# Merging four heads at a time, three merges in flight, and a lag of four units in a dilated-attention layer on one Trainium2 core

## The chip, the cores and the metric

The kernel runs on one core of a Trainium2 chip. The metric is the device time in microseconds of one execution, and the time given is the median of several executions. TensorE is called PE in the profile's rows, VectorE DVE, ScalarE ACT, GpSimd POOL, SyncE SP; PEld is TensorE's loading of weights. All DMAs that the kernel starts are issued from SP's queue.

## The reference, cut to what matters

Two layers work on 1,024 tokens of width 1,024. The first (mixer A) is a dilated sliding-window attention with 16 heads of 64. For each of three groups (window, dilation) it computes queries, keys and values, rotates queries and keys, and takes a banded softmax over tokens strided by the dilation. The three groups' results are then merged by their softmax denominators, multiplied by a SiLU gate and projected:

```python
for gi, (window, dil) in enumerate(((128, 1), (512, 4), (2048, 16))):
    q, k, v = ...
    o, lse = banded_attention(strided(q), strided(k), strided(v), window // dil)
    outs.append(o); lses.append(lse)
wts = softmax(stack(lses), axis=0)
o = einsum('gbsh,gbshd->bshd', wts, stack(outs))
return (o * silu(z)) @ w_out
```

Then `x <- LayerNorm(alpha * x + mixer(x))` and `x <- x + sigmoid(x Wg) * (p Wp)`. The second layer (mixer B) is a sliding-window attention with shared keys and values, a learned sink per head, the same kind of gate and the same ending; it has no merge.

## The kernel before, in words

Every large product is taken as three fp16 products of high and low halves (lines 272 to 274): a tile of 128 tokens by 512 columns is 24 matmuls into one bank of PSUM (`lin`). Weight blocks are loaded (L102), measured (L109, then a 128x128 diagonal `mdd`, a matmul at L237 and a maximum) and split into halves `whl` (L132 on ScalarE, L133 on VectorE), a step at a time, between the tiles that use the block before. The block of the output projection's second half is split into `wo`, in a pool that opens when layer A's attention pool `att` has closed, on the same memory.

Layer A (`layer_a`) runs over two pairs of head quarters, and in each over the groups 1, 2, 0. A group begins with eight tiles of values (`v_out`) for eight heads, then has two blocks (`i` = 0, 1) of eight tiles of queries and keys for four heads each. A query-key tile is rotated with the group's tables `cos` and `sin` (L347, L350 on VectorE, L351 on POOL), split (L357, L358, L361) and transposed by a DMA into `qk` (L362). It then queues a *unit* of four heads: `score` (matmuls L385, masked maxima L389, exponentials L395, halves L399 and L401, a DMA transpose into `pT` at L404), and `value` (matmuls L416 to L418 into one of two halves of the PSUM tile `o`, then ScalarE's copy into `st` at L698, and a DMA of `st` to the scratch tensor `scr` in DRAM at L707). `unit_step` starts one unit's scores and computes the weighted values of the unit `lag` steps before; there are as many `pT` buffers as the lag and one more `st`. `upt` sets how many units a tile brings.

When group 0 of a head quarter pair has its values for a token tile, a `merge` is queued: it loads the three groups' results for eight heads (`gt`, L749), finds the weights from their maxima and sums (L754 to L762, with one exponential on ScalarE, L756), weighs and adds the three on POOL (L765 to L767) and VectorE (L769, L770), and writes the result to `o_dr` (L771, named `oa` in rows). At most two merges are under way, and `merge_every` says after how many tiles each advances by a step.

The gate `z` of layer A is 16 tiles (`z_tile`, L720 to L723) after the last group. Then `mixed` reads the merged rows and the gate (L898, L899), multiplies them on POOL (L902), scales, splits and transposes them (L878, `ogT`), and runs the output projection as tiles of `lin` from `ogT`.

The order of each engine's instructions is laid out ahead by a planner that plays the program on a timeline of its own (`schedule_with_timeline_sim=True`). An instruction goes where the planner thinks its inputs and buffers are ready, with the program's order as priority; each engine, and SP's queue, then takes its list in order. So a merge's loads can stand far ahead of their place in the program: the first `gt` load of the trace is issued at 261 us, when group 1 of the first pair has been written.

## Time and profile before

| what | us |
|---|---|
| median of 3 runs | 1657.37 (1656.64 to 1660.12) |
| the profiled execution | 1658.17 |
| its span, first to last instruction | 1656.4 |
| TensorE busy | 1587.8 (96%) |
| VectorE busy | 1078.1 (65%) |
| ScalarE busy | 922.7 (56%) |
| POOL busy | 664.6 (40%) |
| mean granted clock of TensorE | 0.985 of full speed |

A busy share is a mean over stages. Layer A with its gate lasts from about 75 to 1055 us, its ending to 1225, layer B the rest. A wait in the rows is named by what ended it, in brackets behind the instruction that waited; times of instructions are from the start of the span.

### The profile page before, as it was taken

What the parts mean: (1) busy time and instruction counts of PE and PEld (TensorE: products, weight loads), DVE (VectorE), ACT (ScalarE), POOL (GpSimd) and SP (SyncE); (2) the same over time, 40 slices, a digit from 0 to 9 for tenths busy, and PEclk for the clock granted to TensorE, in tenths of its full rate; (3) what the DMA queues carried; (4) which work ended last, traced back from release to release, by engine and by line L of the source; (5) the groups of instructions that cost most, each with busy time, mean ns of one, the idle gap of its engine ahead of it and who ended that gap; (6) DMA issues with size and microseconds to landing.
All of it is one profiled execution on the core that took longest, in us unless ns stands there. A gap on an engine that the chain in (4) does not pass through costs nothing. (4 is left out here: it accounts for less than half of the span.)

```text
span 1656.4 us, 29029 instructions
## 1 busy us (share of the span) xinstructions
PE 1587.8 (96%) x10579; PEld 883.2 (53%) x10579; DVE 1078.1 (65%) x2619; ACT 922.7 (56%) x2050; POOL 664.6 (40%) x477
## 2 busy tenths in 40 slices
PE   9999999999999799999999988899999998999998
PEld 3455676654555456666545543344455555544444
DVE  6866655655566776556466567887447998677731
ACT  4537665675774467656657843533334878754321
POOL 0015624532554665155235653453323452225341
PEclk9999999999999999999999998999999999999999
DMA  9718867775887777567658885989975898998963
GB/s 362 251 61 172 186 135 149 153 158 126 164 159 203 207 170 159 127 157 163 142 124 187 190 226 202 336 221 264 248 185 113 155 206 183 189 297 215 262 197 109
DMA packets 543792, 311.02 MB, mean 188 GB/s; under 512 B 473120, under 2 KB 494240, under 8 KB 543392
## 3 DMA queue, kind: packets, MB, share of 16 engines
q1 hardware_dynamic: 543648, 309.16, 75.3%
q8 instruction: 83, 1.36, 0.3%
q14 instruction: 61, 0.50, 0.1%
HBM read 137.78 MB, written 54.92 MB: 116 GB/s over the span
## 5 line engine op out<-in xcount | busy, mean ns | idle before, releaser
L272 PE MATMUL lin<-whl,xhl 128*128 128x512 f16 x1280 | 488.5, 382 | 2.6 <-ACT zu L722 2.6
L273 PE MATMUL lin<-whl,xhl 128*128 128x512 f16 x1280 | 488.7, 382 | 0.0
L274 PE MATMUL lin<-whl,xhl 128*128 128x512 f16 x1280 | 488.7, 382 | 0.0
L351 POOL TENSOR_TENSOR t<-t,t 128x512 f32<-128x512 f32 (+1 forms) x120 | 153.4, 1278 | 284.8 <-DVE t L350 268.0
L401 POOL TENSOR_TENSOR phl<-sm,phl 128x1024 f16<-128x1024 f32 (+1 forms) x88 | 155.6, 1769 | 233.3 <-ACT phl L399 205.9
L109 DVE TENSOR_REDUCE wpm<-wraw 128x1 f32<-128x1024 f32 (+1 forms) x132 | 156.8, 1197 | 93.6 <-DMA wraw<-in_wa_dram 54.8
L274 PEld LDWEIGHTS <-xhl 128*128 128x128 f16 x1280 | 149.3, 117 | 127.5 <-issue 3.5
L273 PEld LDWEIGHTS <-xhl 128*128 128x128 f16 x1280 | 149.7, 117 | 119.5 <-issue 6.7
L272 PEld LDWEIGHTS <-xhl 128*128 128x128 f16 x1280 | 149.4, 117 | 119.7 <-issue 3.8
L395 ACT ACTIVATE sm<-sm,st,cs 128x128 f32<-128x128 f32 (+1 forms) x384 | 203.6, 532 | 3.6 <-ACT st L393 0.4
L358 POOL TENSOR_TENSOR hl<-t,hl 128x512 f16<-128x512 f32 (+1 forms) x120 | 145.3, 1211 | 131.7 <-ACT hl L357 131.7
L389 DVE CUSTOM_DVE_ANT_0 sm<-s,tab 128x256 f32<-128x256 f32 (+1 forms) x512 | 157.0, 358 | 31.5 <-PE s L385 23.0
L133 DVE SCALAR_TENSOR_TENSOR whl<-wraw,s,whl 128x1024 f16<-128x1024 f32 (+1 forms) x116 | 168.3, 1501 | 12.8 <-ACT whl L132 12.8
L357 ACT ACTIVATE hl<-t 128x512 f16<-128x512 f32 (+1 forms) x120 | 72.3, 602 | 125.4 <-POOL t L351 124.0
L347 DVE TENSOR_TENSOR t<-lin,rope 128x512 f32<-128x512 f32 (+1 forms) x120 | 78.9, 657 | 75.7 <-PE lin L274 41.6
L132 ACT ACTIVATE whl<-wraw,s 128x1024 f16<-128x1024 f32 (+1 forms) x116 | 121.8, 1122 | 5.1 <-DVE s L212 5.0
L272 PE MATMUL lin<-whl,x2T 128*128 128x512 f16 (+1 forms) x320 | 115.5, 361 | 0.0
L273 PE MATMUL lin<-whl,x2T 128*128 128x512 f16 (+1 forms) x320 | 115.2, 360 | 0.0
L274 PE MATMUL lin<-whl,x2T 128*128 128x512 f16 (+1 forms) x320 | 115.0, 359 | 0.0
L399 ACT ACTIVATE phl<-sm 128x1024 f16<-128x1024 f32 (+1 forms) x128 | 110.2, 861 | 1.2
L361 ACT ACTIVATE hl<-hl 128x512 f16<-128x512 f16 (+1 forms) x104 | 63.2, 608 | 54.2 <-POOL hl L358 53.9
L385 PE MATMUL s<-qk 128*128 128x128 f16 x1120 | 81.5, 220 | 9.1 <-DMA qk<-hl 9.1
(187 smaller groups left out, 2883.5 us busy)
## 6 DMA issues: line engine op xcount, KB each, us to landing
wraw<-in_wa_dram SPq DMA_DIRECT2D x56, 512.0 KB, 6.0
scr<-st SPq DMA_DIRECT2D x96, 132.0 KB, 2.3
gt<-scr SPq DMA_DIRECT2D x48, 264.0 KB, 3.4
wraw<-in_wav_dram SPq DMA_DIRECT2D x24, 512.0 KB, 6.4
prh<-pro SPq DMA_DIRECT2D x32, 256.0 KB, 4.1
wraw<-in_wg_dram SPq DMA_DIRECT2D x16, 512.0 KB, 8.7
wraw<-in_wb_dram SPq DMA_DIRECT2D x16, 512.0 KB, 6.4
xg<-y SPq DMA_DIRECT2D x16, 512.0 KB, 3.6
```

Source lines behind the costliest of these rows:

```text
L109: k.nc.vector.tensor_reduce(pm[:, c:c + 1], self.raw[:, c * q:(c + 1) * q], axis=AX.X, op=ALU.max, apply_absolute_value=True)
L132: nc.scalar.activation(hl[:, 0, sl], self.raw[:, sl], AF.Copy, scale=self.s)
L133: self.last = nc.vector.scalar_tensor_tensor(hl[:, 1, sl], self.raw[:, sl], self.s, hl[:, 0, sl], op0=ALU.mult, op1=ALU.subtract)
L272: mm(ps, xh(kt), wh, start=(kt == 0), stop=False)
L273: mm(ps, xh(kt), wl, start=False, stop=False)
L274: mm(ps, xl(kt), wh, start=False, stop=(kt == NK - 1))
L351: nc.gpsimd.tensor_add(t1[:, :nh * HD], t1[:, :nh * HD], t2[:, :nh * HD])
L358: nc.gpsimd.tensor_sub(hl[:, :nh, HD:P], rv, hl[:, :nh, 0:HD])
L389: nc.vector.tensor_tensor_reduce(sm[:, h, :nk], ps[:, i, :nk], mask, 1.0, -3e38, ALU.add, ALU.max, mx[:, h:h + 1])
L395: nc.scalar.activation(sm[:, h, :nk], sm[:, h, :nk], AF.Exp, bias=nbias[:, h:h + 1], scale=cs, accum_out=sums[:, h:h + 1])
L399: nc.scalar.activation(hl[:, 0], sm[:, :, :nk], AF.Copy)
L401: eng.tensor_sub(hl[:, 1], sm[:, :, :nk], hl[:, 0])
```

## The change: four heads per merge, three merges, a lag of four, one rotary buffer

A merge now takes one head quarter (four heads) instead of two, so there are 32 merges with tiles of half the size, and the merges of a pair's first quarter are queued in the first of its two blocks in group 0. Three of them may be under way, and `gt` and `mw` have three buffers. Layer A's lag between scores and weighted values goes from three units to four, with one more `pT` and one more `st` buffer. The rotary tables have one buffer instead of two, and their load stands in the program behind the third value tile instead of ahead of the block.

```diff
@@ -190,7 +190,7 @@
 
     def rope_tables(self, order):
 
-        t = self.const.tile([P, N_ROPE], F32, name="rope", tag="rope", bufs=2)
+        t = self.const.tile([P, N_ROPE], F32, name="rope", tag="rope")
         self.nc.sync.dma_start(t, self.a["tab"][:, order * N_ROPE:(order + 1) * N_ROPE])
         self.cos = t[:, :NT * 32].rearrange("p (n c) -> p n c", n=NT)
         self.sin = t[:, NT * 32:].rearrange("p (n b c) -> p n b c", n=NT, b=2)
@@ -629,7 +629,7 @@
                for i in range(2)]
 
         self.x2_scale()
-        self.set_lag(3)
+        self.set_lag(4)
         self.upt = 0.75
         vh = at.tile([P, 3, NT, 4 * HD], F16, tag="vh", name="vh", bufs=1)
         vl = at.tile([P, 3, NT, 4 * HD], F16, tag="vl", name="vl", bufs=1)
@@ -640,7 +640,6 @@
             for g in (1, 2, 0):
                 if pair and g == 0:
                     self.merge_every = 1
-                self.rope_tables(g)
                 blk = self.next_block()
                 cvs[pair, g] = self.prod(self.invx, blk.inv, 2.0 ** V_SHIFT, "cv")
                 slots = [i for i in range(3) if i != slots[1]]
@@ -648,6 +647,8 @@
                 for n in range(NT):
                     ps = self.ps_lin.tile([P, 512], F32, tag="lin", name="lin")
                     self.lin(ps, blk, *self.stat_a(g, n), 0, 512)
+                    if n == 2:
+                        self.rope_tables(g)
                     self.v_out(ps.rearrange("p (s c) -> p s c", s=2), vh[:, pick, n, :], vl[:, pick, n, :])
                     self.progress()
                 blk.released = True
@@ -705,8 +706,8 @@
             else:
                 d = d[n * P:(n + 1) * P]
             nc.sync.dma_start(d, st)
-            if g == 0 and q % 2:
-                self.merges.append(self.merge(n, q // 2, scr[q // 2]))
+            if g == 0:
+                self.merges.append(self.merge(n, q, scr[q // 2]))
 
         kas = [lambda h, sw, t=qk[i]: t[:, 4 + 4 * sw + h, :] for i in tiles]
         self.later(UNIT_LAG, lambda: self.unit(lambda h: qk[n][:, h, :], kas, mask, cs, ncs,
@@ -741,35 +742,34 @@
             if half == 0:
                 self.w_z.released = True
 
-    def merge(self, n, pair, scr):
+    def merge(self, n, q, scr):
 
         nc, at, sp = self.nc, self.att, self.small
-        gt = at.tile([P, 3, 2, 4 * HD + 8], F32, tag="gt", name="gt")
+        gt = at.tile([P, 3, 4 * HD + 8], F32, tag="gt", name="gt", bufs=3)
         for g in range(3):
-            nc.sync.dma_start(gt[:, g], scr[g][n * P:(n + 1) * P])
-        sums, nb = gt[:, :, :, 4 * HD:4 * HD + 4], gt[:, :, :, 4 * HD + 4:]
+            nc.sync.dma_start(gt[:, g], scr[g][n * P:(n + 1) * P, q % 2])
+        sums, nb = gt[:, :, 4 * HD:4 * HD + 4], gt[:, :, 4 * HD + 4:]
         yield
-        w = sp.tile([P, 3, 2, 4], F32, tag="mw", name="mw")
-        M = sp.tile([P, 2, 4], F32, tag="mM", name="mM")
-        nc.vector.tensor_reduce(M, nb.rearrange("p g a h -> p a h g"), axis=AX.X, op=ALU.min)
-        nc.vector.tensor_sub(w, M.unsqueeze(1).to_broadcast([P, 3, 2, 4]), nb)
+        w = sp.tile([P, 3, 4], F32, tag="mw", name="mw", bufs=3)
+        M = sp.tile([P, 4], F32, tag="mM", name="mM")
+        nc.vector.tensor_reduce(M, nb.rearrange("p g h -> p h g"), axis=AX.X, op=ALU.min)
+        nc.vector.tensor_sub(w, M.unsqueeze(1).to_broadcast([P, 3, 4]), nb)
         nc.scalar.activation(w, w, AF.Exp)
-        wl = sp.tile([P, 3, 2, 4], F32, tag="mwl", name="mwl")
+        wl = sp.tile([P, 3, 4], F32, tag="mwl", name="mwl")
         nc.vector.tensor_mul(wl, w, sums)
-        L = sp.tile([P, 2, 4], F32, tag="mL", name="mL")
-        nc.vector.tensor_reduce(L, wl.rearrange("p g a h -> p a h g"), axis=AX.X, op=ALU.add)
+        L = sp.tile([P, 4], F32, tag="mL", name="mL")
+        nc.vector.tensor_reduce(L, wl.rearrange("p g h -> p h g"), axis=AX.X, op=ALU.add)
         nc.vector.reciprocal(L, L)
-        nc.vector.tensor_mul(w, w, L.unsqueeze(1).to_broadcast([P, 3, 2, 4]))
-        x = [gt[:, g, :, 0:4 * HD].rearrange("p a (h c) -> p a h c", c=HD) for g in range(3)]
-        wb = [w[:, g].unsqueeze(3).to_broadcast([P, 2, 4, HD]) for g in range(3)]
+        nc.vector.tensor_mul(w, w, L.unsqueeze(1).to_broadcast([P, 3, 4]))
+        x = [gt[:, g, 0:4 * HD].rearrange("p (h c) -> p h c", c=HD) for g in range(3)]
+        wb = [w[:, g].unsqueeze(2).to_broadcast([P, 4, HD]) for g in range(3)]
         nc.gpsimd.tensor_mul(x[1], x[1], wb[1])
         nc.gpsimd.tensor_mul(x[2], x[2], wb[2])
         nc.gpsimd.tensor_add(x[1], x[1], x[2])
         yield
         nc.vector.tensor_mul(x[0], x[0], wb[0])
         nc.vector.tensor_add(x[0], x[0], x[1])
-        nc.sync.dma_start(self.o_dr[n][:, pair * 512:(pair + 1) * 512].rearrange("p (a c) -> p a c", a=2),
-                          gt[:, 0, :, 0:4 * HD])
+        nc.sync.dma_start(self.o_dr[n][:, 4 * HD * q:4 * HD * (q + 1)], gt[:, 0, 0:4 * HD])
 
     def merge_step(self):
 
@@ -777,7 +777,7 @@
         if self.merge_wait > 0:
             return
         self.merge_wait = self.merge_every
-        while len(self.merging) < 2 and self.merges:
+        while len(self.merging) < 3 and self.merges:
             self.merging.append(self.merges.pop(0))
         for m in list(self.merging):
             if next(m, "end") == "end":
```

## Rows read from the trace of the kernel before

**Rows 1.** The page's first part: busy time of each engine in us, its share of the span, and its number of instructions.

```profile
PE 1587.8 (96%) x10579; PEld 883.2 (53%) x10579; DVE 1078.1 (65%) x2619; ACT 922.7 (56%) x2050; POOL 664.6 (40%) x477
```

**Rows 2.** TensorE's waits over the whole span: the instruction that waited, what it waited for, us in total, times, the longest.

```profile
PE s L237 <- DVE mdd L230: 15.6, 3, 7.3
PE s L385 <- DMA qk<-hl: 9.1, 5, 3.1
PE o L416 <- DMA pT<-phl: 8.1, 5, 3.7
PE o L416 <- ACT st L698: 7.9, 4, 4.4
```

**Rows 3.** The timeline of TensorE, its longer stalls in and behind layer A, two weighted values (975.95, 981.83) and the first projection stall of layer B: start in us, us of the instruction (or the run of equal ones), and in brackets the idle time before it and what ended that.

```profile
527.62 0.19 PE L416 MATMUL o<-vh,pT 128*128 128x64 f16 x1 [2.17 <-ACT st L698]
...
551.35 0.21 PE L416 MATMUL o<-vh,pT 128*128 128x64 f16 x1 [4.45 <-ACT st L698]
...
574.65 1.07 PE L385 MATMUL s<-qk 128*128 128x128 f16 x16 [3.12 <-DMA qk<-hl]
...
956.19 0.73 PE L385 MATMUL s<-qk 128*128 128x128 f16 x10 [1.47 <-DMA qk<-hl]
960.66 0.24 PE L416 MATMUL o<-vh,pT 128*128 128x64 f16 x1 [3.73 <-DMA pT<-phl]
...
975.95 0.19 PE L416 MATMUL o<-vh,pT 128*128 128x64 f16 x1
...
981.83 0.19 PE L416 MATMUL o<-vh,pT 128*128 128x64 f16 x1
...
1028.40 0.29 PE L237 MATMUL s<-mdd,ones 128*128 128x128 bf16 x1 [4.89 <-DVE mdd L230]
...
1054.14 0.29 PE L237 MATMUL s<-mdd,ones 128*128 128x128 bf16 x1 [7.33 <-DVE mdd L230]
1054.67 0.59 PE L272 MATMUL lin<-whl,ogT 128*128 128x512 f16 x1 [0.24 <-PE s L237]
...
1484.63 0.29 PE L237 MATMUL s<-mdd,ones 128*128 128x128 bf16 x1 [3.35 <-DVE mdd L230]
```

**Rows 4.** Windows: the stretch, its length in us, the busy us (and instructions) of PE, PEld, DVE, ACT and POOL, the granted clock of TensorE (1.00 is full speed), the DMA engines' busy share, GB/s.

```profile
505.00:590.00 85.00, 72.79 (x518) 41.45 (x517) 63.99 (x164) 38.77 (x99) 52.49 (x38) 0.94 0.73 189
...
860.00:936.00 76.00, 75.06 (x652) 42.13 (x651) 44.78 (x135) 58.68 (x146) 43.86 (x30) 1.00 0.83 168
936.00:986.00 50.00, 44.79 (x369) 24.38 (x367) 33.41 (x83) 31.53 (x72) 26.13 (x17) 0.93 0.94 235
986.00:1029.00 43.00, 35.51 (x158) 15.57 (x157) 28.21 (x59) 10.91 (x18) 18.86 (x15) 0.94 0.56 191
1029.00:1055.00 26.00, 18.43 (x74) 7.60 (x73) 18.43 (x40) 18.98 (x25) 8.42 (x6) 0.83 0.98 335
1055.00:1140.00 85.00, 79.48 (x354) 35.05 (x353) 72.44 (x149) 29.50 (x33) 39.23 (x22) 0.96 0.94 255
```

**Rows 5.** The timeline of SP's queue: the last write of `scr`, the last three loads of `gt`, the last two outputs of merges; start and us of issuing.

```profile
985.92 0.38 SPq L707 DMA_DIRECT2D scr<-st  x1
...
1007.97 1.27 SPq L749 DMA_DIRECT2D gt<-scr  x3
...
1023.95 3.42 SPq L771 DMA_DIRECT2D oa<-gt  x2
```

**Rows 6.** The timeline of ScalarE at one of the stalls of rows 3, and where `wo` opens in layer A and in layer B.

```profile
546.08 0.22 ACT L756 ACTIVATE mw<-mw 128x24 f32<-128x24 f32 x1 [2.34 <-DVE mw L755]
...
546.69 4.25 ACT L132 ACTIVATE whl<-wraw,s 128x1024 f16<-128x1024 f32 x4
550.85 0.46 ACT L698 ACTIVATE st<-o,cv 128x256 f32<-128x256 f32 x1
...
1029.40 4.26 ACT L132 ACTIVATE wo<-wraw,s 128x1024 f16<-128x1024 f32 x4 [10.74 <-DMA oa<-gt]
...
1459.83 2.19 ACT L132 ACTIVATE wo<-wraw,s 128x1024 f16<-128x1024 f32 x2 [3.96 <-DMA ob<-mu]
```

**Rows 7.** The tile `gt`: who waited for its instructions, us in total and times.

```profile
  ACT mw L756: 54.6, 14
  DVE mM L754: 27.5, 11
```

**Rows 8.** Groups of instructions by line and shape: busy us, mean ns of one, and the idle time before them with what ended it.

```profile
L351 POOL TENSOR_TENSOR t<-t,t 128x512 f32<-128x512 f32 x112 | 149.8, 1337 | 275.8 <-DVE t L350 259.9 <-DVE m L218 9.9 <-DVE mdt L226 2.7
...
L765 POOL TENSOR_TENSOR gt<-gt,mw 128x512 f32<-128x512 f32 x16 | 23.6, 1477 | 58.3 <-DVE mw L762 56.7 <-DMA gt<-scr 1.3
...
L770 DVE TENSOR_TENSOR gt<-gt 128x512 f32<-128x512 f32 x16 | 17.8, 1113 | 7.9 <-POOL gt L767 7.8
...
L755 DVE TENSOR_TENSOR mw<-mM,gt 128x24 f32<-128x24 f32 x16 | 4.8, 302 | 0.3
...
L351 POOL TENSOR_TENSOR t<-t,t 128x128 f32<-128x128 f32 x8 | 3.6, 454 | 9.0 <-DVE t L350 8.1 <-DVE inv L211 0.5 <-DVE m L218 0.4
```

**Rows 9.** DMA issues: what, from where, number, KB each, median us from issue to landing.

```profile
scr<-st SPq DMA_DIRECT2D x96, 132.0 KB, 2.3
gt<-scr SPq DMA_DIRECT2D x48, 264.0 KB, 3.4
...
rope<-in_tab_dram SPq DMA_DIRECT2D x7, 384.0 KB, 3.7
```

## The prediction

> **What bounds the kernel now.** I read the page first. TensorE is busy for 1587.8 us, 96% of the span [rows 1], so only what keeps it waiting, or slows it, can be won. The list of its waits [rows 2] has no large item: 15.6 us for the diagonal `mdd` of a weight block's maximum, 9.1 us for `qk` transposes, 8.1 us for `pT` transposes, 7.9 us for ScalarE to empty `o`. So I asked where they lie. The timeline of TensorE [rows 3] puts nearly all of layer A's into two places: 527 to 575 us, where the weighted values of the first head pair end and its merges run, and 956 to 1055 us, where the same happens for the second pair and the output projection must start. In windows [rows 4], 505 to 590 holds 85 - 72.79 = 12.2 us of idle TensorE at a granted clock of 0.94; 936 to 1055 holds 119 - (44.79 + 35.51 + 18.43) = 20.3 us at 0.93, 0.94 and 0.83. A clock under 1 means that part of the window ran at the lower level (1.2 GHz instead of 2.4), after a stall each time. Taking the missing share of the window as lost time, 505 to 590 loses another 0.06 x 85 = 5.1 us, and 936 to 1055 loses 0.07 x 50 + 0.06 x 43 + 0.17 x 26 = 10.5 us.
>
> What do these stalls have to do with merges? At 551.35 TensorE waits 4.45 us for ScalarE's `st` (L698) [rows 3]; ScalarE had sat 2.34 us for a merge's `mw`, then did the 4.25 us of a weight split, and only then `st` [rows 6]. Over the kernel ScalarE waits 54.6 us (14 times) for L755 of a merge, and VectorE 27.5 us (11 times) for a merge's load [rows 7]. In the second place the chain is longer. The last weighted values start at 981.83 [rows 3] and the last `scr` write is issued at 985.92, but the last merge's loads are issued at 1007.97 and its output at 1023.95 [rows 5]. ScalarE then stands 10.74 us before `wo`, whose memory a merge's `gt` still holds, until 1029.40 [rows 6]. The first tile of the output projection starts at 1054.67 [rows 3], 25.3 us after that. Layer B has no merges, and there the same distance is 1484.63 - 1459.83 = 24.8 us [rows 3, 6]. So 25 us behind the opening of `wo` is the pace of that stage, and the merges set when it opens.
>
> **The change part by part.**
>
> *Smaller merges.* 16 merges of eight heads become 32 of four. Those of the first four heads of a pair can start one block of eight tiles earlier, so at the end only eight small ones are left.
>
> What each costs: VectorE and ScalarE's small steps stay as many per merge; six on VectorE at no more than L755's 0.30 us [rows 8] make 1.8 us, so 16 more merges add at most 29 us to VectorE, which is 65% busy. On POOL, L351 takes 1.337 us for 512 elements and 0.454 for 128 [rows 8], 2.3 ns per element, so 256 fewer take 0.59 us off each of three operations like L765 (1.477): at most 3 x 0.89 = 2.7 us instead of 4.4. Of L770's 1.11 us about 0.6 stays. A load of 132 KB lands in 2.3 us by `scr<-st`, one of 264 KB in 3.4 [rows 9].
>
> The chain of the last merge, after: the last weighted values come one z tile later (next part, 5.9 us), so `scr` is issued at 985.92 + 5.9 = 991.8 and lands 2.3 later; three loads take 1.3 to issue and 2.3 to land (997.7); the small steps with the exponential 2.0; POOL 2.7; L770 0.6; the output 0.4 + 2.3. That is 1005.7, against 1029.4 now. With 25.3 us to the first projection tile: 1031.0 instead of 1054.67, a gain of 23.7. TensorE allows it: its work from 936 to 1055, without idle time and at full clock, is 119 - 20.3 - 10.5 = 88.2 us, which ends at 1024. Bounds: 0 if the last merge ends no earlier, 30 us if TensorE alone sets the stage. I take 21, near the chain, because the load in front of it meets transposes in SP's queue.
>
> In 505 to 590 half of the merge work moves out. At most 12.2 + 5.1 = 17.3 us are won there, nothing at least; I take half, 9. From 1055 to 1140 there are 85 - 79.48 = 5.5 us of idle and 0.04 x 85 = 3.4 of clock [rows 4], rows late behind the same opening. They start earlier, but so does TensorE: 0 to 8.9, I take 2.
>
> The price: 16 small merges now run in 425 to 505 and 860 to 936, among scores and rotations. What hides them is TensorE's work and slack on VectorE. If each cost what one of the eight did in 505 to 590, scaled by its half size, it would be 17.3 / 8 / 2 = 1.1 us, 17.5 in all; if the planner's order holds, nothing. I take 5.
>
> *Three under way.* Three `gt` buffers of half size: a load waits for the output of the third merge before it, not the second. That wait is what put the last loads 22 us behind the last `scr` write. If it is back, the gain of 21 goes. The 48 more loads and 16 more outputs all go through SP's queue, past `qk` and `pT` transposes: at 0.42 us each (1.27 for three [rows 5]) 27 us, spread over 500.
>
> *Lag of four.* It gives each `pT` one unit more to land (the 3.73 at 960.66 [rows 3] is such a wait) with one more `pT` and `st` buffer. It moves the last weighted values by one z tile, the distance from 975.95 to 981.83, 5.9 us, counted above. What is queued behind a `pT` wait is all of TensorE. The waits for `o` aren't touched by it: those need ScalarE.
>
> *One rotary buffer.* A load now waits for the last rotation of the group before, on SP. Its next reader is eight value tiles later (at 5.9 us each, 47 us) and it lands in 3.7 us [rows 9]. Nothing, unless the planner puts it too early on SP: then transposes wait behind it for a tile at most. At most 5.9 x 6 = 35 us by this, at least nothing; I take nothing, as the distance is ten times the landing.
>
> Sum: 21 + 9 + 2 - 5 = 27 us. The profiled execution took 1658.2 us, so 1631; the median of the runs, 1657.4, lies 0.8 lower, within what the runs scatter. Forecast 1631.
>
> **A rule against it.** The row says that half the bytes land in 2.3 instead of 3.4 us [rows 9], so two halves, one after the other, cost 1.2 us more than one whole. The Trainium skill, "DMA: Bandwidth & Descriptors", "Anatomy of one DMA", gives a fixed part of about 2 us per transfer whatever its size, and its "Rules for kernel authors" say to coalesce many small transfers. By its formula (2.0 us plus bytes at 436 GB/s, an estimate) the load falls only from 2.6 to 2.3 us, and the last merge would end 0.8 us later than by the difference of my rows. The trace agrees that halving the bytes does not halve the time.
>
> **The rivals.**
>
> *The merges end early, but the next stage doesn't follow.* Weight loads, row transposes or the z tiles hold the first projection tile; layer B, where TensorE still waits 3.35 us at 1484.63 [rows 3], speaks for some of this, the equal 25 us of both layers against it. Then only about half of the 27 comes: 1645.
>
> *The loads' fixed price eats it.* 48 more loads, each half landing 2.3 - 3.4 / 2 = 0.6 us later than half a whole, make 29 us if nothing hides them. 27 won and 29 lost: 1660 at the worst, about 1657 if a little is hidden. Against it: only 11 of 16 merges' loads were waited for, 2.5 us each. This is the case of no change; that the planner already sets the starts, and the change does little, ends here too. The rule on coalescing points to this one.
>
> *Slower.* Each merge is a place where VectorE and ScalarE, which take their work in order, can stand for a load or for each other, and the 16 added ones fall where scores need both. At the unscaled price of 505 to 590, 17.3 / 8 = 2.2 us each, they cost 35 us, and the eight left in that place keep costing what they did. Against the 23 won at the end of the layer: 1658 + 35 - 23 = 1670. It decides from 23 / 16 = 1.4 us per added merge. For it: ScalarE is busy 58.68 of 76 us in 860 to 936 [rows 4]. Against: that window, which has the same units, shows only 0.9 us of idle TensorE.
>
> **How the numbers follow.** Forecast 0.56 (1618 to 1643 by itself), next stage doesn't follow 0.19, no change 0.09, slower 0.16. Faster than now by over 0.2% (3.3 us, about what a measurement can tell from no change): 0.75; within it 0.09; slower 0.16. The range takes in the first two and half of the third: 1616 to 1657.
>
> **What would show it.** In the profile after: `gt` loads in 32 groups of three, those of the first four heads of each pair's last group before 505 and 930 us; the last output of a merge near 1005 less what was won before; ScalarE's 10.74 us before `wo` at the same distance of 25 us from the first projection tile, but 20 us earlier; the waits of 4.89 and 7.33 us for `mdd` shorter; the clock in that stretch above 0.95. The sum is wrong if TensorE shows new waits for `st` or `qk` in 425 to 505 or 860 to 936, or if the last merge still ends 40 us behind the last weighted values.

## The result and the profile after

The changed kernel takes 1675.35 us in the median, against 1658.51 us of the kernel before beside it: 1.0109 times as long, with a 95% interval of 1.0095 to 1.0122. One of its four executions took 2449.18 us at a granted clock of 0.63, and the ratio is taken without it. The forecast was 1631. The time was lost where none was forecast to be, and the gain at the end of the layer did not come.

The page's first part, for the kernel after, answers to [rows 1]:

```profile
PE 1593.2 (95%) x10579; PEld 885.0 (53%) x10579; DVE 1117.3 (67%) x2747; ACT 922.9 (55%) x2066; POOL 667.8 (40%) x525
```

TensorE has 5.4 us more busy time; the rest of the 17.3 us by which the span is longer is waiting. VectorE has 39 us more. TensorE's waits over the whole span, as [rows 2]:

```profile
PE o L416 <- ACT st L699: 23.2, 13, 3.6
PE s L385 <- DMA qk<-hl: 8.8, 5, 2.8
PE lin L272 <- DMA ogT<-rhl: 7.6, 2, 4.0
PE s L237 <- DVE p2e L205: 7.2, 1, 7.2
PE s L237 <- DVE mdd L230: 3.5, 1, 3.5
```

The waits for ScalarE to empty `o` (L699, which was L698) have trebled, from 7.9 us to 23.2. The waits for `pT` shrank from 8.1 us to 3.1, and those of the maximum's product (L237), which stand under `mdd` and `p2e`, from 15.6 to 10.7. Where the longer ones lie, from the timeline of TensorE, as [rows 3]:

```profile
475.88 0.19 PE L416 MATMUL o<-vh,pT 128*128 128x64 f16 x1 [2.78 <-ACT st L699]
498.13 0.19 PE L416 MATMUL o<-vh,pT 128*128 128x64 f16 x1 [3.57 <-ACT st L699]
...
526.21 0.19 PE L416 MATMUL o<-vh,pT 128*128 128x64 f16 x1 [2.47 <-ACT st L699]
...
975.11 1.14 PE L385 MATMUL s<-qk 128*128 128x128 f16 x9 [2.78 <-DMA qk<-hl]
1004.90 0.19 PE L416 MATMUL o<-vh,pT 128*128 128x64 f16 x1 [3.26 <-ACT st L699]
1048.56 0.29 PE L237 MATMUL s<-mdd,ones 128*128 128x128 bf16 x1 [7.21 <-DVE p2e L205]
1063.06 0.38 PE L272 MATMUL lin<-whl,ogT 128*128 128x512 f16 x1
...
1120.63 0.39 PE L272 MATMUL lin<-whl,ogT 128*128 128x512 f16 x1 [3.96 <-DMA ogT<-rhl]
1136.53 0.39 PE L272 MATMUL lin<-whl,ogT 128*128 128x512 f16 x1 [3.62 <-DMA ogT<-rhl]
1181.52 0.38 PE L272 MATMUL lin<-whl,xgT 128*128 128x512 f16 x1 [3.36 <-ACT gth L980]
```

The stalls at 475.88 and 498.13 are new: that stretch had none. The first product of the output projection starts at 1063.06 instead of 1054.67, and waits for row transposes (`ogT`) lie inside that stage. Windows of the kernel after, as [rows 4], with one more stretch in front:

```profile
430.00:505.00 75.00, 68.65 (x556) 39.06 (x555) 63.01 (x149) 48.63 (x112) 48.34 (x43) 0.98 0.90 186
505.00:590.00 85.00, 75.81 (x552) 42.68 (x550) 63.22 (x174) 41.49 (x107) 39.58 (x40) 0.94 0.70 177
860.00:936.00 76.00, 75.13 (x612) 41.47 (x610) 55.59 (x153) 54.29 (x138) 48.40 (x40) 1.00 0.88 178
936.00:986.00 50.00, 40.02 (x343) 22.62 (x343) 37.74 (x116) 32.84 (x81) 30.12 (x27) 0.93 0.99 231
986.00:1029.00 43.00, 39.74 (x241) 19.17 (x240) 25.02 (x70) 18.64 (x38) 18.87 (x22) 0.96 0.64 180
1029.00:1055.00 26.00, 18.79 (x79) 7.97 (x77) 22.31 (x36) 13.27 (x19) 11.52 (x6) 0.87 0.95 332
1055.00:1140.00 85.00, 76.04 (x347) 33.91 (x345) 71.89 (x142) 33.69 (x38) 31.66 (x20) 0.98 0.86 229
```

The same first stretch in the kernel before, where TensorE had no idle time at all:

```profile
430.00:505.00 75.00, 75.00 (x627) 42.67 (x626) 50.18 (x113) 53.35 (x120) 40.94 (x26) 1.00 0.86 180
```

How a merge makes TensorE wait there is to be read from four timelines of the kernel after, put in order of time:

```profile
471.67 2.12 POOL L401 TENSOR_TENSOR phl<-sm,phl 128x1024 f16<-128x1024 f32 x1
471.81 2.26 DVE L771 TENSOR_TENSOR gt<-gt 128x256 f32<-128x256 f32 x1
473.75 1.44 POOL L351 TENSOR_TENSOR t<-t,t 128x512 f32<-128x512 f32 x1
474.00 0.15 DVE L755 TENSOR_REDUCE mM<-gt 128x4 f32<-128x12 f32 x1
474.19 1.04 DVE L756 TENSOR_TENSOR mw<-mM,gt 128x12 f32<-128x12 f32 x1
475.26 0.21 ACT L757 ACTIVATE mw<-mw 128x12 f32<-128x12 f32 x1 [2.88 <-DVE mw L756]
475.38 0.46 ACT L699 ACTIVATE st<-o,cv 128x256 f32<-128x256 f32 x1
475.88 0.19 PE L416 MATMUL o<-vh,pT 128*128 128x64 f16 x1 [2.78 <-ACT st L699]
```

ScalarE stands 2.88 us, from 472.38 on, at the merge's exponential. Until 474.07 VectorE is still at the last sum of another merge (L771), which takes 2.26 us here and 0.42 in the median of the 32. Then its subtraction of 12 elements takes 1.04 us, and 0.17 where no GpSimd operation runs beside it. Each of the two ends at most 0.3 us behind the GpSimd operation beside it. Only behind the exponential comes the copy that empties `o`, and TensorE waits for that. Over the kernel ScalarE waits 58.5 us, 24 times, for L756 (54.6 and 14 in [rows 7]).

### The profile page after: what moved, and what is told of

Its sections match the earlier page's. It is cut to its first block, busy times and chain, and to the rows that moved or that the text cites. A ratio compares the mean times of both kernels' runs of the same rounds, so it can differ in the third digit from the quotient of the medians.

```text
span 1673.7 us, 29337 instructions
## 1 busy us (share of the span) xinstructions
PE 1593.2 (95%) x10579; PEld 885.0 (53%) x10579; DVE 1117.3 (67%) x2747; ACT 922.9 (55%) x2066; POOL 667.8 (40%) x525
## 5 line engine op out<-in xcount | busy, mean ns | idle before, releaser
L109 DVE TENSOR_REDUCE wpm<-wraw 128x1 f32<-128x1024 f32 (+1 forms) x132 | 157.0, 1197 | 89.5 <-DMA wraw<-in_wa_dram 48.7
L347 DVE TENSOR_TENSOR t<-lin,rope 128x512 f32<-128x512 f32 (+1 forms) x120 | 78.7, 656 | 70.0 <-PE lin L274 42.4
L417 PEld LDWEIGHTS <-pT 128*128 128x128 f16 x800 | 72.0, 99 | 45.7 <-issue 36.6
```

What stands on the lines that cost most here:

```text
L109: k.nc.vector.tensor_reduce(pm[:, c:c + 1], self.raw[:, c * q:(c + 1) * q], axis=AX.X, op=ALU.max, apply_absolute_value=True)
```

## The experiments

All times below are medians, and "over" is the distance from the median of the kernel before in the same set. Three marks in the traces tell where time went: the start of VectorE's rotation (L347) of the 40th and of the 88th query-key tile, at 432.4 and 880.8 us before, and the end of the last product of layer A's output projection, at 1147.2. Between the first two lies all of the first pair's merging, between the last two all of the second pair's and the opening of the next stage. Each of the last two columns is how much longer that stretch is than before. The marks are those of one profiled execution, which can lie some us beside the median (that of e14 took 1665.65 us, 9 more than its median; that of e7 1670.87, 6 less).

| kernel | median | over | 40th to 88th | 88th to last product |
|---|---|---|---|---|
| the change | 1675.35 | +16.8 | +8.8 | +2.8 |
| e1: merges alone | 1673.98 | +14.8 | +4.7 | +3.5 |
| e2: without the lag of four | 1673.24 | +14.1 | +5.6 | +3.0 |
| e3: even quarter queued with the odd | 1675.14 | +16.0 | +3.8 | +10.8 |
| e4: no exponential | 1670.58 | +11.4 | +4.3 | +4.6 |
| e5: exponential with bias | 1677.77 | +19.9 | +8.9 | +13.8 |
| e7: merges without GpSimd | 1676.90 | +19.0 | +8.9 | +5.0 |
| e6: no arithmetic, 32 merges | 1652.92 | -5.0 | -9.9 | +0.2 |
| e12: no arithmetic, 16 merges | 1639.06 | -17.9 | -17.0 | -6.9 |
| e13: arithmetic in the first pair | 1671.58 | +14.6 | +11.4 | +3.4 |
| e14: arithmetic in the second pair | 1656.69 | -0.3 | -8.0 | +4.9 |
| e10: small merges in the second pair | 1675.91 | +18.0 | +2.7 | +13.3 |
| e11: small merges in the first, late | 1671.48 | +14.5 | +7.1 | -1.7 |
| e15: one load, 32 merges | 1687.85 | +29.2 | +14.6 | +9.8 |
| e16: one load, 16 merges | 1664.09 | +5.4 | -1.8 | -0.3 |
| e17: before, transfers halved | 1669.85 | +11.2 | +1.5 | +7.2 |
| e18: merges on GpSimd's queue | 1694.29 | +35.0 | +10.3 | +20.7 |
| e19: weights on GpSimd's queue | 1689.38 | +30.1 | +10.4 | +22.1 |
| e20: loads in reverse order | 1685.18 | +25.6 | +13.3 | +13.8 |

The last row is the yardstick for all others, so it comes first.

**How far a new order alone moves the time (e20).**

```diff
-        for g in range(3):
+        for g in (2, 1, 0):
             nc.sync.dma_start(gt[:, g], scr[g][n * P:(n + 1) * P, q % 2])
```

> The changed kernel with the three loads of each merge issued in the order 2, 1, 0 instead of 0, 1, 2: the same transfers, the same arithmetic, nothing that should cost or save time by itself, but the planner that orders each engine's list orders some two thousand of TensorE's rows anew. It measures how far a new order alone moves the time, and so how much of a few microseconds in the other experiments means anything. If the order hardly matters: within 3 us of the changed kernel (1672 to 1679). If a new order alone moves the time as much as the experiments do: 6 us or more away on either side.

Measured: 1685.18 us, ratio 1.0147 (1.0126 to 1.0168), 9 us beyond the change. Same transfers, same arithmetic; the planner orders every engine's list anew, and its waits fall elsewhere. From the list of TensorE's waits of this kernel:

```profile
PE o L416 <- ACT st L699: 24.0, 11, 4.1
PE s L385 <- DMA qk<-hl: 14.1, 5, 6.7
PE s L237 <- DVE mdd L230: 12.6, 3, 6.8
```

The item for `st` is what it was, those for `qk` and `mdd` are 5 and 9 us longer. So between two kernels whose lists differ, 9 us may mean nothing but another order, and only larger differences, or the same sign over many kernels, carry a verdict below. This is one reordering of one kernel: its 9 us are a size to go by and no bound, and that the reversed loads cost nothing by themselves is taken for granted here.

**Which part of the change costs: e1 and e2.** e1 is the kernel before with the change's merges, lag of three and two rotary buffers; e2 is the change with a lag of three.

```diff
 e1, against the kernel before: merge() and unit_a() as in the change, and
-        while len(self.merging) < 2 and self.merges:
+        while len(self.merging) < 3 and self.merges:
 e2, against the change
-        self.set_lag(4)
+        self.set_lag(3)
```

> The kernel before with the small merges alone: four heads, three under way, the even quarters' merges early; lag of three, two rotary buffers. The changed kernel takes 1675 us, the one before 1658. Theory A (the added merges make VectorE and ScalarE stand in stretches where scores need them; lag and rotary buffer do nothing): 1671 to 1678. Theory B (lag of four costs as well as the merges, or alone): 1662 or less. Theory C (the lag helped and hides part of the merges' price): 1680 or more.

> The changed kernel with the lag back at three, one rotary buffer kept. With the run of small merges alone it tells the lag from the rotary buffer. Theory A: 1671 to 1678, as the merges are the cost. Theory B (the lag delays the last weighted values by a z tile and costs): 1669 or less. Theory C: 1680 or more, with more waits of TensorE for pT.

Measured: 1673.98 (1.0093, 1.0064 to 1.0123) and 1673.24 (1.0092, 1.0063 to 1.0121). Both are where theory A had them. The merges alone bring the loss, all but 2 us of it. Without the lag of four, and without lag and rotary buffer, the time stays within 3 us of the change, which the yardstick can't tell from nothing.

**Later start: e3.**

```diff
             if g == 0:
-                self.merges.append(self.merge(n, q, scr[q // 2]))
+            if g == 0 and q % 2:
+                self.merges += [self.merge(n, i, scr[q // 2]) for i in (q - 1, q)]
```

> The changed kernel, but the merges of an even quarter are queued together with those of the odd one, so that none of the 32 runs in the two blocks in which TensorE fell behind by 13 and 10 us (448 to 503 and 912 to 940 us). Theory A1 (the place is what costs: small merges among scores and rotations): those 23 us go; the 12 us won at the end of layer A shrink, since 16 small merges are now left there: 1652 to 1664. Theory A2 (the number of merges is what costs, wherever they run): 1671 to 1680, the loss moved behind 503 and 940 us.

Measured: 1675.14 (1.0099, 1.0072 to 1.0125). The stretch from the 40th to the 48th tile, 12.9 us longer in the change, is 0.7 shorter here: one merge's output is issued before 505 us instead of five. But nine instead of five outputs are issued after 1000 us, TensorE waits 26.25 us for `mdd` at 1070.84, and the end is where it was. The time is that of theory A2: the early loss is real and can be moved; it comes back behind.

**The chain over ScalarE and GpSimd: e4, e5 and e7.** e4 leaves out the exponential (L757), e5 puts the subtraction into it, e7 takes GpSimd out of the merge.

```diff
 e4
-        nc.scalar.activation(w, w, AF.Exp)
 e5
-        nc.vector.tensor_sub(w, M.unsqueeze(1).to_broadcast([P, 3, 4]), nb)
-        nc.scalar.activation(w, w, AF.Exp)
+        for h in range(4):
+            nc.scalar.activation(w[:, :, h], nb[:, :, h], AF.Exp, scale=-1.0, bias=M[:, h:h + 1])
 e7
-        nc.gpsimd.tensor_mul(x[1], x[1], wb[1])
-        nc.gpsimd.tensor_mul(x[2], x[2], wb[2])
-        nc.gpsimd.tensor_add(x[1], x[1], x[2])
+        nc.vector.tensor_mul(x[1], x[1], wb[1])
+        nc.vector.tensor_mul(x[2], x[2], wb[2])
+        nc.vector.tensor_add(x[1], x[1], x[2])
```

> The changed kernel without the merge's exponential (L757 is left out, so the groups are weighted by the exponent itself; all else runs). ScalarE then has nothing of a merge in its list. Theory S (TensorE's new waits for st come from ScalarE standing at L757 for VectorE, with the copies of o behind it): the 23 us of the two blocks fall to under 8, waits for st from 23 us to under 5: 1650 to 1660. Theory Q (SP's queue with 64 more transfers, or VectorE itself, holds TensorE): 1668 to 1677, with qk waits in their place.

> The changed kernel, but the merge's subtraction on VectorE and its exponential on ScalarE (one each of 12 elements) become four exponentials on ScalarE with the minimum as bias and scale -1, so no 12-element subtraction can be held behind a GpSimd operation, and ScalarE waits for the minimum alone, whose instruction has one input and never ran longer than 0.17 us. Theory A (the early blocks lose because ScalarE stands at the merge's exponential while VectorE's subtraction is held behind GpSimd): the 23.2 us in which TensorE waited for the copy of L699 fall to under 12, the shift at the 48th query-key tile falls from 11.6 to under 6, and the time to 1668 or less. Theory B (the place and the waits of the merges on the lists matter, not this one subtraction): the time stays within 1672 to 1680, with 64 times 3 more exponentials on ScalarE, and the shift at that tile stays above 9.

> The changed kernel, but the weighing and adding of the merge's second and third part (two products and a sum of 128x256) move from GpSimd to VectorE: no GpSimd work is left in a merge, and VectorE gets 3 instructions of about 0.42 us each more, 1.3 us a merge, 40 us in all. Theory A (VectorE and GpSimd holding each other up is what the 32 merges cost): the merge's subtraction of L756 keeps near 0.2 us more often, its total falls from 19.0 to under 12 us, and the time falls to 1660 to 1668. Theory B (VectorE's own load is what counts in these blocks): VectorE gains 40 us of work and the time rises to 1680 or more.

Measured: 1670.58 (1.0076, 1.0052 to 1.01), 1677.77 (1.0128, 1.0103 to 1.0153), 1676.90 (1.0126, 1.0095 to 1.0158). None recovers the loss, and the stretch from the 40th to the 48th tile stays 11.5, 11.4 and 15.0 us longer. TensorE's waits for `st`, 23.2 us in the change, are 11.3, 20.1 and 17.8; in e4 those for `qk` are 16.3 instead of 8.8. By their times e4 and e5 fall to the theories against the chain, and e7 between its two. In e7 the subtraction's total halves, from 19.0 to 9.4 us, but the merge's two other small products (L759, L763) take 31.9 instead of 26.0: the rest of GpSimd's work still runs beside them. VectorE's merge work grows from 98 to 144 us, yet the time is the change's within the yardstick. So the chain shown above is how single stalls come about; cut at any one place it gives back some 5 us at most (e4). What all the hold-ups of VectorE cost together none of the three tells.

**The arithmetic, by pairs: e6, e12, e13 and e14.** e6 and e12 keep each merge's loads and output, in the change and in the kernel before, and leave its arithmetic out. e13 and e14 do that for one pair of the change.

```diff
 e6 and e12: everything between the loads and the output
+        yield
+        yield
 e13 (e14: q < 2)
+        out = self.o_dr[n][:, 4 * HD * q:4 * HD * (q + 1)]
+        if q > 1:
+            yield
+            yield
+            nc.sync.dma_start(out, gt[:, 0, 0:4 * HD])
+            return
```

> The changed kernel with the merges' arithmetic left out: each merge still makes its three loads and, two steps on, its store, but nothing on VectorE, ScalarE or GpSimd. It separates SyncE's queue and the transfers from the engines. Theory A (the engines' share costs): the shift at the 48th query-key tile (11.6 us in the changed kernel) and at the 96th (18.0) falls to 0 or below, since even the 16 merges of the kernel before are gone, and the time falls to about 1640 to 1650. Rival (64 more transfers on SyncE's queue and the DMA engines delay the scores' stores and the tables): the shifts stay above 6 and the time above 1660.

> The kernel before with the arithmetic of its merges of eight heads left out: the loads and the store of each merge remain, on the same steps. If the end of the merges bounds the end of the attention stage, as the prediction has it, the last merge ends some 20 us earlier and the first product of the projection's stage starts about 20 us before 1054.7 and the time falls by 20 us or more, to 1640 or less. Rival (the stage has another bound close behind, and the changed kernel without arithmetic shows no gain after 880 us for this reason): the last product of the projection moves by at most 8 us against its place at 835 us, and the time is 1645 to 1655.

> The changed kernel with the arithmetic of the second pair's sixteen merges left out (loads and stores remain). Theory (the loss of the first pair stays to the end): the time lies 12 to 20 us above that of the kernel without any arithmetic (1652.9), at 1665 to 1673. Rival (the first pair's loss is made good later, since another chain bounds the stage of the projection): at most 6 us above, under 1659.

> The changed kernel with the arithmetic of the first pair's sixteen merges left out (loads and stores remain). Theory (the pairs add up): the changed kernel's 22 us above the kernel without any arithmetic are split, 16 from the first pair and 6 from the second, so 1657 to 1661. Rival (the second pair's merges alone bring the loss, as in the experiment that changed the second pair alone): 1668 or more.

Measured: 1652.92 (0.9973, 0.9955 to 0.9991), 1639.06 (0.9894, 0.9865 to 0.9923), 1671.58 (1.0095, 1.0079 to 1.0111), 1656.69 (1.0001, 0.9984 to 1.0017). e6 lies 3 us above what theory A gave, e14 0.3 below; e12 and e13 fall where their theories had them.

In the change, the first pair's arithmetic costs 14.6 + 5.0 = 19.6 us and the second pair's 5.0 - 0.3 = 4.7; together 24.3 against 16.8 + 5.0 = 21.8 for both. The pairs add up. In the kernel before, all arithmetic costs 17.9, 17.0 of it before the 88th tile. So the arithmetic of 32 small merges is 3.9 us dearer than that of 16 large ones, and the other 12.9 us lie between e6 and e12, two kernels without arithmetic: in loads, outputs, the places where they stand, the lag and the rotary buffer. That is little more than the yardstick. So although e14 shows that without the first pair's arithmetic the loss is gone, that arithmetic does not set the change apart from the kernel before, which pays nearly as much for its own (17.0 us against 19.6).

e12 also tells what the tail could give at most. With no merge arithmetic at all, the first projection product starts at 1020.9, 33.8 us earlier, of which 16.5 were won before the 88th tile; yet the stretch from the 88th tile to the last product is only 6.9 us shorter, and with the yardstick's 9 on top still short of the 21 forecast: the projection now takes 102.9 us instead of 92.5. So the time is the one that the theory of its expectation gave (1640 or less), but 17.0 us of it are won ahead of the 88th tile. The projection of the kernel before:

```profile
1054.70:1147.20 92.50, 86.98 (x387) 38.35 (x388) 77.44 (x159) 32.32 (x36) 41.59 (x24) 0.97 0.95 255
```

Windows of e12, 25 us ahead of the first product and the projection:

```profile
996.00:1020.90 24.90, 23.14 (x107) 10.05 (x106) 24.66 (x43) 13.93 (x19) 9.55 (x6) 1.00 0.91 292
1020.90:1123.80 102.90, 90.19 (x388) 39.29 (x389) 85.20 (x170) 40.40 (x46) 41.61 (x24) 0.93 0.90 234
```

and of the change:

```profile
1038.00:1063.10 25.10, 17.89 (x75) 7.57 (x74) 23.80 (x43) 13.65 (x20) 11.52 (x6) 0.86 0.92 270
1063.10:1157.40 94.30, 85.34 (x389) 38.16 (x388) 79.69 (x159) 35.75 (x39) 38.55 (x24) 0.98 0.89 239
```

VectorE (the third number after the length) is busy 24.66 of 24.90 us in e12 and 23.80 of 25.10 in the change: in e12 the maxima of weights (L109) take 8.4 us of it, the split of `wo` 5.9 and the gate rows 4.2. TensorE itself is busy 23.14 of these 24.90 us. Ahead of them VectorE had stood for weights:

```profile
994.54 2.48 DVE L109 TENSOR_REDUCE wpm<-wraw 128x1 f32<-128x1024 f32 x2 [9.44 <-DMA wraw<-in_wg_dram]
...
1000.55 0.16 DVE L212 RECIPROCAL s<-inv 128x1 f32<-128x1 f32 x1
...
1000.80 4.27 ACT L132 ACTIVATE wo<-wraw,s 128x1024 f16<-128x1024 f32 x4 [3.65 <-DVE cw L927]
```

`wo` is split by the scale `s` of its block (L212). VectorE comes to that scale only behind the maxima of the next block's weights, the gate's, for which it waits 9.44 us, and `wo` opens 0.09 us after it, 17.1 us after the last merge output has landed. This is what stands behind the merges. The projection that starts earlier takes more of VectorE's work into itself (85.20 us against 77.44 before) and is 10.4 us longer; that the one makes the other is not shown.

**Small merges in one pair only: e10 and e11.** Both are the kernel before, with merges of eight heads kept in the other pair, lag three, two under way (`merge8` is the merge of the kernel before); e11 queues both quarters' merges behind the odd one.

```diff
             if g == 0 and q % 2:
-                self.merges.append(self.merge(n, q // 2, scr[q // 2]))
 e10
+            if g == 0 and q == 1:
+                self.merges.append(self.merge8(n, 0, scr[0]))
+            if g == 0 and q > 1:
+                self.merges.append(self.merge(n, q, scr[1]))
 e11
+            if g == 0 and q == 1:
+                self.merges += [self.merge(n, i, scr[0]) for i in range(2)]
+            if g == 0 and q == 3:
+                self.merges.append(self.merge8(n, 1, scr[1]))
```

> The kernel before, with its merges of eight heads kept for the first pair of quarters and merges of four heads, two under way, for the second pair alone; lag 3 and two rotary buffers as before. If the loss adds up by blocks: no loss at the 48th query-key tile (11.6 us in the changed kernel, within 2 of 0 here), but still 8 to 10 us more between the 88th and the 96th, and the time 1664 to 1670. If it does not add up, because the loss of the first pair is made good by the 32nd value tile anyway: 1672 or more.

> The kernel before with one change: the first pair's eight merges of eight heads become sixteen merges of four heads, all queued where the merges of eight heads were, after the odd quarter's units; the second pair keeps its merges of eight heads, two under way. Theory (the first pair loses because the even quarter's merges begin in the stretch 430 to 505, where TensorE had no idle time in the kernel before; queued later, merges of four heads cost nothing and fill the idle time of 505 to 590): 4 us earlier than before at the 56th query-key tile, as in the experiment that queued all merges late (4.3), and a time of 1652 to 1658. Rival (32 smaller merges cost by their number, wherever they are): 4 us or more later at that tile and 1662 or more.

Measured: 1675.91 (1.0119, 1.0088 to 1.0149) and 1671.48 (1.0087, 1.0066 to 1.0109), both on the side of their rivals. By its marks e10 has no loss up to the 48th tile and 8.9 us between the 88th and the 96th, as the theory of adding up wanted, but more is lost behind. It is no faster than the change although half of that is undone: its 13.3 us lie behind the 88th tile, with one stall of 13.93 us at 1064.82 for ScalarE's row split. In e11, with two merges under way, the first pair's outputs go on to 655.7 us, where they ended at 587.7, into a stretch where TensorE had been busy 268 of 270 us. Small merges are not cheap in either pair, and the two don't add up.

**The transfers: e15, e16 and e17.** One load for three (the scratch of the groups as one tensor), in the change and in the kernel before; and the kernel before with each load and the output in two halves.

```diff
 e15 (e16: the same, without q % 2)
-        for g in range(3):
-            nc.sync.dma_start(gt[:, g], scr[g][n * P:(n + 1) * P, q % 2])
+        nc.sync.dma_start(gt, scr[n * P:(n + 1) * P, :, q % 2])
 e17
-            nc.sync.dma_start(gt[:, g], scr[g][n * P:(n + 1) * P])
+            for i in range(2):
+                nc.sync.dma_start(gt[:, g, i], scr[g][n * P:(n + 1) * P, i])
```

> The changed kernel, but the scratch of the three groups is one tensor and each merge of four heads fetches its rows of all three with one load instead of three: 64 loads fewer on SyncE's queue, the same bytes, the same arithmetic. Theory Q (the number of transfers on SyncE's queue is what doubling the merges costs: 48 more loads and 16 more stores stand ahead of the rotations' and the probabilities' transposes): at most 3 us later than before at 880 us, and 1657 to 1665. Theory E (the arithmetic on the engines and where it stands costs): 1671 or more.

> The kernel before with the same one load in place of three for its merges of eight heads: 32 loads fewer on the queue, the same bytes. Theory Q: 5 to 9 us faster than before, 1648 to 1652. Theory E: the time of before, within 4 us.

> The kernel before with the transfers alone of the change: its merges of eight heads, their arithmetic and their place stay, but each of the three loads and the store is cut in two halves of four heads, 48 loads and 16 stores more, the same bytes. Theory Q: 8 to 14 us slower than before, 1665 to 1671, with TensorE waiting longer for the transposes of L362 and L404. Theory E: the time of before, within 4 us, and the 14 us between the two kernels without arithmetic come from the earlier start of the even quarter's merges and their steps.

Measured: 1687.85 (1.0175, 1.0149 to 1.02), 1664.09 (1.003, 1.0015 to 1.0045), 1669.85 (1.0065, 1.0041 to 1.0089). Doubling the transfers alone costs 11.2 us, as theory Q said; taking two loads in three away costs 12.5 and 5.4 us, against it. The Trainium skill has many small transfers coalesced into one large one ("DMA: Bandwidth & Descriptors", "Rules for kernel authors"); e17 agrees with it, e15 and e16 don't, and next to the yardstick of 9 us none of the three decides; e16 lies outside both of its theories.

**Another queue: e18 and e19.**

```diff
 e18: the merges' loads and outputs
-            nc.sync.dma_start(gt[:, g], scr[g][n * P:(n + 1) * P, q % 2])
+            nc.gpsimd.dma_start(gt[:, g], scr[g][n * P:(n + 1) * P, q % 2])
 e19: four weight blocks
+            queue = k.nc.gpsimd if 20 <= k.blocks.index(self) < 24 else k.nc.sync
```

> The changed kernel with the merges' 96 loads and 32 stores issued from GpSimd's queue instead of SyncE's: the same transfers, but nothing of the merges stands ahead of the transposes or the weight loads on SyncE's queue. Theory Q (the place on SyncE's queue is what the additional transfers cost): the four loads of the first output-projection block, which in the kernel before begin at 889.7 to 905.1 us and in the changed kernel at 896.8 to 920.5, end no later against their first than before (15.4 us, 23.7 in the changed kernel), and the time is 1660 to 1668. Theory D (the DMA engines, 99% busy from 880 to 960 us against 85.6% before, are full whichever queue issues): 1672 or more.

> The changed kernel with the loads of four weight blocks alone (both of the output projection and both of the gate) issued from GpSimd's queue, so that they no longer stand behind the merges' transfers on SyncE's queue. Theory W (the weights of the next stage, prepared one block after another, are what ends late there): the four loads of the first block begin within 18 us of each other, the split of the second output-projection block on ScalarE begins before 1028 us instead of at 1036.1, and the time is 1661 to 1668. Rival (the weights are not the bound, other work of the stage is): the split comes earlier but the time stays at 1672 or more.

Measured: 1694.29 (1.0209, 1.0177 to 1.0241) and 1689.38 (1.0186, 1.016 to 1.0213). In e19 the four loads of the first projection block begin within 6.6 us of each other, at 897.3 to 903.9, as theory W wanted, but the split of that block on ScalarE begins at 1022.2 instead of 1017.2 and that of the second at 1045.2 instead of 1036.1. So the second sign of theory W did not come, and neither did that of its rival, which had the split earlier. This does not clear the weights: the gate's loads, which in the change are issued at 1024.62 to 1027.39, are issued at 1032.25 to 1037.76 on GpSimd's queue, VectorE stands 3.99 us for them, and `wo` opens 0.08 us after its scale here too. A run that brings the gate's weights earlier was not made. In e18 the stretch from the 40th to the 48th tile is 16.2 us longer, the longest of all, though no merge stands on SyncE's queue: the early loss comes without them there too. Neither run separates the queue from the DMA engines, since the transfers are slower on GpSimd's queue (from 880 to 960 us a load of 132 KB lands in 4.0 us there in e18, in 2.7 on SyncE's queue in the change).

What the DMA engines did from 880 to 960 us, as share of all sixteen, in the kernel before and then in the change:

```profile
q1 hardware_dynamic: 38479, 15.05, 85.6%
```

```profile
q1 hardware_dynamic: 40295, 16.18, 99.0%
```

They are full in that stretch after the change. Whether that costs time there no run showed.

## Why the prediction was wrong

The forecast took 27 us off, and 16.8 came on. By the marks, the stretch up to the 88th tile was to shrink by 9 less half of the 5 for added merges, 6.5 us, and grew by 8.8; from there to the last projection product 21 + 2 less 2.5, 20.5 us, and it grew by 2.8. Another 4.8 us came in the gate's stage, by the stall at 1181.52; of the experiments only e14 loses as much there, so I count it to the order. That is 43.4 of the 44 us between forecast and result.

*The last merge's chain: right.* The forecast had its output issued 1003.0 - 987.7 = 15.3 us behind the last weighted values. It is issued at 1021.04, the values start at 1004.90: 16.1 us. In the kernel before it was over 42 ([rows 3, 5]). With three buffers the last load waits for its own scratch write (until 1012.97) and not for a buffer. But the last values came 17.2 us later than forecast.

*What the end of the merges is worth: wrong, the largest error.* The step was "the merges set when it opens". From the timelines of SyncE's queue, VectorE and ScalarE of the kernel after, put in order of time:

```profile
1021.04 0.32 SPq L772 DMA_DIRECT2D oa<-gt  x1
...
1024.62 1.13 SPq L102 DMA_DIRECT2D wraw<-in_wg_dram  x2
...
1031.57 1.22 DVE L109 TENSOR_REDUCE wpm<-wraw 128x1 f32<-128x1024 f32 x1 [5.77 <-DMA wraw<-in_wg_dram]
...
1034.15 0.28 DVE L239 TENSOR_REDUCE m<-s 128x1 f32<-128x128 f32 x1
...
1035.88 0.15 DVE L212 RECIPROCAL s<-inv 128x1 f32<-128x1 f32 x1
1036.11 4.27 ACT L132 ACTIVATE wo<-wraw,s 128x1024 f16<-128x1024 f32 x4 [1.92 <-DMA za<-zu]
```

`wo` now opens 15.1 us behind the last output and no longer within 5.5 ([rows 5, 6]). It opens 0.08 us after the scale of its own block is ready. The bracket names a store of gate rows (`za`), but the two in question landed at 1033.49 and 1036.67. The scale is late because VectorE's maximum of the `wo` block (L239) stands in its list behind the maxima of the gate's weights (L109), for which VectorE waits 5.77 us; their load waits for the buffer that the split of the block before frees at 1024.6. The trace of the kernel before had the sign of it:

```profile
1027.75 0.16 DVE L212 RECIPROCAL s<-inv 128x1 f32<-128x1 f32 x1
```

There the scale was ready at 1027.9, 1.5 us before `wo` opened at 1029.40. An earlier end of the merges was worth these 1.5 us, unless the scale came earlier too. The profiled executions of all twenty kernels agree: in thirteen `wo` opens within 0.1 us after the scale, in the other seven, the kernel before among them, within 0.3 us after the last merge output has landed. e2 shows what this means: with the lag of three the last output is issued 4.6 us earlier than in the change (1016.48), but the last product ends where it did (1157.6 against 1157.4).

The pace of 25 us from there to the first product was 27.0 in the change (1063.06 - 1036.11); over the twenty kernels it is 19.9 to 31.6, so it was no fixed pace. Two layers with the same distance did not show that nothing else stood just behind the merges. The rival that the next stage doesn't follow had the mechanism, and weight loads were the first that it named. Its time, 1645, was still too low, since even without arithmetic (e12) the whole stretch gives only 6.9 us.

*505 to 590 us: direction right, a third of the size.* TensorE's idle time fell from 12.2 to 85 - 75.81 = 9.2 us at the same clock, 3.0 won and not 9. I had half of the work move out; only five of sixteen outputs are issued before 505 us, eleven stay.

*The price of the added merges: the sign that it would show was named, the size was not.* New waits for `st` between 425 and 505 us were to show the sum wrong, and they stand at 475.88 and 498.13. That stretch loses 75 - 68.65 = 6.35 us of idle time and 0.02 x 75 = 1.5 of clock, 7.9 us, more than the 5 for all sixteen. Where I had looked for cover, in 860 to 936, TensorE is as busy as before (75.13 against 75.06). The cover was missing in 430 to 505, which the forecast didn't look at: 75.00 of 75 us busy means that there is no idle time to hide a stall in. The slack on VectorE was mis-sized as well: 16 more merges were to add 29 us at most, at 0.30 us for each small step, and VectorE has 39 more. The three small steps with two inputs (L756, L759, L763) grew from 4.8 + 3.7 + 4.1 = 12.6 us in 16 merges to 45.0 in 32. (The forecast's bound of 17.5 us for the 16 is 17.3: 17.3 / 8 / 2 times 16.)

*1055 to 1140: wrong sign, small.* 8.96 us idle and 0.02 x 85 = 1.7 of clock, 10.7 against 8.9: 1.8 lost, 2 forecast won.

*Lag and rotary buffer: nothing to be told* of the time from e1 and e2, as forecast for the buffer. Of the 5.9 us for the lag, 4.6 are seen at the last merge's output (e2, above) and none at the end of the projection.

*The rivals.* "Slower" gave 1670 and had the chain by which TensorE waits. Its sum was another: 35 us lost and 23 won, where neither figure came. The fixed price of loads was put at up to 29 us; e17 measured 11.2 for the same number of transfers, not far above the yardstick. The formula that the prediction takes from the Trainium skill ("DMA: Bandwidth & Descriptors", "Anatomy of one DMA") is given there for DMAs issued from GpSimd, and this kernel's come from SyncE's queue. The change's loads of 132 KB land in 2.6 us in the median where those of 264 KB landed in 3.4: 0.8 less, between the formula's 0.3, an estimate, and the 1.1 of [rows 9]. VectorE's waits for merge loads grew from 27.5 us in 11 places to 36.6 in 20.

*What is shown and what stays open.* Shown: the merges bring the loss (e1); eleven kernels with all 32 small merges and arithmetic, or nearly all of it, are 11 to 35 us slower than before, in whatever order; the first pair's arithmetic costs 15 us more than the second's (e13, e14), as nearly all of it falls there in the kernel before (e12); what opens `wo` behind the merges (the traces); that the tail gives some 7 us, the yardstick's 9 on either side, when all merge arithmetic goes (e12). Not settled: why the projection takes longer when it starts earlier, and how the 13 us between e6 and e12 divide among transfers, their earlier places and mere order. Of the versions with all the arithmetic none is faster than the kernel before.

## What to carry to other kernels

Before a gain is booked for removing the last thing that a stage waits for, leave its work out altogether and time that: here it gave some 7 us where 21 were booked. And look in the trace before for what the stage waits for next to last: here it was ready 1.5 us ahead of the last. Work that is moved earlier needs idle time where it lands; a window in which TensorE is busy 75.00 of 75 us takes none. Where a planner orders the lists, time a reordering that changes nothing else, and trust no difference below what it makes.

## What the runs showed of the hardware

A GpSimd operation holds up even VectorE's smallest two-input instructions. From the timelines of the kernel after:

```profile
459.09 2.32 POOL L401 TENSOR_TENSOR phl<-sm,phl 128x1024 f16<-128x1024 f32 x1
459.41 2.03 DVE L756 TENSOR_TENSOR mw<-mM,gt 128x12 f32<-128x12 f32 x1
...
462.71 0.17 DVE L756 TENSOR_TENSOR mw<-mM,gt 128x12 f32<-128x12 f32 x1
```

Twelve elements a partition take 0.17 us alone and 2.03 behind a GpSimd operation; over the 32 merges the line's mean is 0.593 us, its longest 2.067:

```profile
L756 DVE TENSOR_TENSOR mw<-mM,gt 128x12 f32<-128x12 f32 x32 | 19.0, 593 | 0.7
L759 DVE TENSOR_TENSOR mwl<-mw,gt 128x12 f32<-128x12 f32 x32 | 13.4, 418 | 6.0 <-ACT mw L757 6.0
L763 DVE TENSOR_TENSOR mw<-mw,mL 128x12 f32<-128x12 f32 x32 | 12.6, 394 | 0.7
```

Of the 96 instructions of these three lines 35 are lengthened, and each of the 35 ends within 0.15 us of the end of a GpSimd operation. The reduction L755 of the same merges, with one input, takes 0.15 to 0.17 us in all 32, also in the 13 that lie wholly within a GpSimd operation. The Trainium skill has the rule ("SBUF — State Buffer", "SBUF: two separate sides"): the port pair that GpSimd and VectorE share is an "exclusive lock" and "not a bandwidth split", and of VectorE's ordinary operations those with two inputs in SBUF need it. The trace agrees. The prediction priced these instructions at no more than 0.30 us each by [rows 8], without it. How much of the kernel's loss is this lock's stays open: e7 took half of the subtraction's time away, but of the three lines together only 45.0 - 41.3 = 3.7 us.
